# The eleven bf16 data sums of the MID node, on GpSimd or on VectorE

## The chip, the cores and the metric

The kernel runs on one core of one Trainium2 chip. The metric is the device time of one launch in microseconds (us). "Before" ran at 779.34 us, the median of 2 runs (779.1 to 779.57). Each run has a state by its granted TensorE clock and its time; only fast runs are compared. A ratio below is the mean time of one kernel's fast runs over the mean of the other's fast runs of the same rounds on the same chip, so it is not quite the ratio of the medians that are quoted.

## The reference, cut to what matters

```python
# x: [8, 4096, 512] f32, kernel: [8, 512, 512] f32
out = np.zeros_like(x)
for k in range(8):
    shifted = x if k == 0 else concatenate([zeros(B, k, D), x[:, :-k]], axis=1)
    out += np.matmul(shifted, kernel[k])
```

It is a causal convolution of eight taps whose weights are 512x512 matrices.

## The kernel before

Each of the 128 partitions holds a run of 256 consecutive time steps, taken in 32 rounds of eight. Eight taps on eight steps would be 64 matrix products. Three nested levels of a Karatsuba-like scheme need fewer. A round has three nodes, MID, LO and HI. Each has nine products of four 128x128 by 128x512 matmuls on sums of input blocks: the D tiles in the code, in bf16. The sums at the level of the data cost no matmul but a pass of an elementwise engine.

```python
    def tt(o, a, b, op):
        nc.vector.tensor_tensor(out=o, in0=a, in1=b, op=op)

    def load(out, src):
        nc.gpsimd.dma_start(out=out, in_=src)        # f32 in HBM to bf16 in SBUF

    def load_x(i, h):                                 # two buffers in all
        xin[i, h] = xpool.tile([P, 4, D], bf, name="xin")
        load(xin[i, h], xr[:, K * i + 4 * h:K * i + 4 * h + 4, :])

    def transpose_x(i, h):
        nc.sync.dma_start_transpose(out=XT[:, 4 * h:4 * h + 4, :]..., in_=xin[i, h]...)

    def prep_m():                                     # MID's D1 (2 sums), D2[1:5] (4 sums)
        tt(D1[:, 0:2], XT[:, 7::-7], XT[:, 0:2], ADD)
        tt(pairs(D2[:, 1:5]), pairs(XT)[:, 3::-3], pairs(XT)[:, 0:2], ADD)

    def prep_d27():                                   # D2[0], 1 sum
        tt(D2[:, 0], XT[:, 5], XT[:, 7], ADD)

    def prep_d21():                                   # D21, 4 sums, MID's last level
        tt(D21[:, 0:4], D2[:, 0:4], D2[:, 1:5], ADD)
    # ... prep_d4, prep_d41, prep_d42, prep_d421: the same for LO and HI
```

The steady loop, one node a pass:

```python
    for k, (i, a) in enumerate(order):                # MID, LO, HI of each i
        # ...
        if a == MID and more:
            transpose_x(i + 1, 0)                     # first transpose of the next round
        node_l(cur, 0, LO)                            # MID: reads D21[0]
        node_l(cur, 0, HI)
        # ... a0 and u products of the next node
        node_l(cur, 1, LO)
        node_e(cur, 0)                                # output: ACT copy in MID, else VectorE + store
        # ... ACT seeds the next node's PSUM banks
        if a == MID:
            prep_d421(LO)
            prep_d41(HI)
        elif a == LO:
            if more:
                prep_m()
            prep_d421(HI)
        elif more:
            prep_d41(LO)
            prep_d42(LO)
            prep_d21()
        # ... v products of the next node, and the two differences (VectorE, PSUM)
        if a == MID:
            prep_d42(HI)
            prep_d27()
        elif more:
            prep_d4(LO if a == LO else HI)
        node_l(cur, 1, HI)
        # ... a1 product of the node after the next: reads D1 when that is MID
        node_e(cur, 1)
        if a == LO and more:
            transpose_x(i + 1, 1)                     # second transpose of the next round
            if i + 2 < NIT:
                load_x(i + 2, 0)                      # overwrites what transpose (i+1, 0) read
                load_x(i + 2, 1)                      # overwrites what transpose (i+1, 1) read
```

Before, GpSimd's queue held only the loads in the steady loop.

Of the kernel before, what the change touches and what calls it, by code (L numbers as in the profile page):

```python
# [22 lines left out]
def kernel(  # L23
# [6 lines left out]
    nc = tc.nc  # L30
# [44 lines left out]
    def tt(o, a, b, op):  # L75
        nc.vector.tensor_tensor(out=o, in0=a, in1=b, op=op)  # L76
# [7 lines left out]
    def load_x(i, h):  # L84
# [4 lines that stand above are left out]
        nc.sync.dma_start_transpose(  # L89
            out=XT[:, 4 * h:4 * h + 4, :].rearrange("p j (c m) -> p (j c) m", m=P),  # L90
            in_=xin[i, h].rearrange("p j d -> p (j d)"))


    def pairs(z):
        return z.rearrange("p (a b) d -> p a (b d)", b=2)

    def prep_m():

        tt(D1[:, 0:2], XT[:, 7::-7], XT[:, 0:2], ADD)
        tt(pairs(D2[:, 1:5]), pairs(XT)[:, 3::-3], pairs(XT)[:, 0:2], ADD)  # L100

    def prep_d27():
        tt(D2[:, 0], XT[:, 5], XT[:, 7], ADD)

    def prep_d21():
        tt(D21[:, 0:4], D2[:, 0:4], D2[:, 1:5], ADD)

    def prep_d4(h):
        a, b = (XT[:, 4:8], XT[:, 0:4]) if h == LO else (XT[:, 0:4], XT[:, 4:8])
        tt(D4[:, 4 * h:4 * h + 4], a, b, ADD)  # L110

    def prep_d41(h):
        if h == LO:
            tt(D41[:, 0:2], D4[:, 7::-7], D4[:, 0:2], ADD)
        else:
            tt(D41[:, 2:4], D4[:, 3:5], D4[:, 4:6], ADD)

    def prep_d42(h):
        if h == LO:
            tt(pairs(D42)[:, 0:2], pairs(D4)[:, 3::-3], pairs(D4)[:, 0:2], ADD)  # L120
        else:
            tt(D42[:, 4:8], D4[:, 2:6], D4[:, 4:8], ADD)

    def prep_d421(h):
        if h == LO:
            tt(D421[:, 0:4:2], D42[:, 7:0:-6], D42[:, 0:4:2], ADD)
            tt(D421[:, 1:4:2], D42[:, 0:4:2], D42[:, 1:4:2], ADD)
        else:
            tt(D421[:, 4:8], D42[:, 3:7], D42[:, 4:8], ADD)
# [106 lines left out]
    def node_a1(k):  # L236
        n = Node()
        nodes.append(n)
        n.k, (n.i, n.a) = k, order[k]
        a = n.a  # L240
        n.s = streams(n.i, a)
        n.q = pair(3)
        product(n.q[:, 1], n.s[1][1], W[a, MID, HI], True)
        nc.scalar.copy(out=n.q[:, 0], in_=n.q[:, 1])  # L244
        n.p = {}

    def node_a0(n):
        product(n.q[:, 0], n.s[1][0], W[n.a, MID, LO], False)

    def node_u(n):  # L250
        product(n.q[:, 1], n.s[0], W[n.a, MID, MID], False)

    def node_seed(n, b_):
        n.p[b_] = pair((2 * n.k + b_) % 3)
        if b_ == LO:
            nc.scalar.copy(out=n.p[b_][:, 1], in_=n.q[:, 1])  # L256
        else:
            nc.scalar.mul(out=n.p[b_][:, 1], in_=n.q[:, 1], mul=-1.0)  # L258

    def node_dts(n):  # L260
        n.dts = cpool.tile([P, D], f32, name="dts")
        nc.scalar.copy(out=n.dts, in_=n.q[:, 0])  # L262

    def node_v(n, b_):
        product(n.p[b_][:, 1], n.s[2][b_], W[n.a, b_, MID], False)

    def node_d(n, b_):
        p = n.p[b_]
        if b_ == LO:
            tt(p[:, 0], n.dts, p[:, 1], SUB)  # L270
        else:
            nc.vector.scalar_tensor_tensor(out=p[:, 0], in0=p[:, 1], scalar=-1.0,  # L272
                                           in1=n.dts, op0=MUL, op1=SUB)
# [3 lines left out]
    def node_l(n, b_, j):  # L277
        product(n.p[b_][:, j], n.s[3][2 * b_ + j], W[n.a, b_, j], False)
# [11 lines left out]
    def node_e(n, b_):  # L290
        p = n.p[b_]
        if n.k < 4:
            pool, name = ((mpool, "ms"), (ypool, "y"), (fpool, "f"), (ypool, "y"))[n.k]
            y = pool.tile([P, 2, D], f32, name=name)
            nc.scalar.copy(out=y, in_=p)  # L295
            first[n.i, n.a, b_] = y
        elif n.a == MID:
            ms[b_] = mpool.tile([P, 2, D], f32, name="ms")
            nc.scalar.copy(out=ms[b_], in_=p)  # L299
        else:  # L300
            y = ypool.tile([P, 2, D], f32, name="y")
            if b_ == HI and n.k == len(order) - 1:

                for j, eng in enumerate((nc.scalar, nc.sync)):
                    tt(y[:, j], p[:, j], ms[b_][:, j], ADD if n.a == LO else SUB)
                    eng.dma_start(out=orr[:, K * n.i + 4 * n.a + 2 * b_ + j, :], in_=y[:, j])
            else:
                tt(y, p, ms[b_], ADD if n.a == LO else SUB)
                store(n.i, n.a, b_, y)
# [111 lines left out]
    node_u(nodes[1])  # L421
    node_e(nodes[0], 0)
    prep_d27()
    mid_dve(2, HI, LO)
    load_w(1)
# [88 lines left out]
    node_l(nodes[4], 0, LO)  # L514
    node_u(nodes[5])
    prep_m()
    node_d(nodes[4], 1)
    node_y(nodes[4], 0, LO)
# [8 lines left out]
    node_dts(nodes[5])  # L527
    node_v(nodes[5], 0)
    prep_d27()
    node_seed(nodes[5], 1)  # L530
    node_y(nodes[4], 1, LO)
# [42 lines left out]
    for k, (i, a) in enumerate(order):  # L574
        if k < 6:
            continue
        cur = nodes[k]
        more = i + 1 < NIT
        if a == MID and more:
            transpose_x(i + 1, 0)  # L580
        node_l(cur, 0, LO)
        node_l(cur, 0, HI)
        nxt = nodes[k + 1] if k + 1 < len(order) else None
        if nxt:
            node_a0(nxt)
            node_u(nxt)
        node_l(cur, 1, LO)
        node_e(cur, 0)
        if nxt:
            node_seed(nxt, 0)  # L590
            node_seed(nxt, 1)
            node_dts(nxt)
        if a == MID:
            prep_d421(LO)
            prep_d41(HI)
        elif a == LO:
            if more:
                prep_m()
            prep_d421(HI)
        elif more:  # L600
            prep_d41(LO)
            prep_d42(LO)
            prep_d21()
        if nxt:
            for b_ in range(2):
                node_v(nxt, b_)
                node_d(nxt, b_)
        if a == MID:
            prep_d42(HI)
            prep_d27()  # L610
        elif more:
            prep_d4(LO if a == LO else HI)
        node_l(cur, 1, HI)
        if k + 2 < len(order):
            node_a1(k + 2)
        node_e(cur, 1)
        if a == LO and more:
            transpose_x(i + 1, 1)
            if i + 2 < NIT:
                load_x(i + 2, 0)  # L620
                load_x(i + 2, 1)
# [30 lines left out]
```

## Time and profile before

| | before |
|---|---|
| time | 779.34 us |
| TensorE busy | 99% |
| VectorE busy | 85% |
| GpSimd busy | 5% |
| granted TensorE clock | 1.00 |
| a steady round | 23.32 us |

Busy shares say which engine has no room; they don't say which wait ends last. For this, read the chain that ended last and the waits. A row of groups reads: line, engine, operation, output from input, shapes, count, then busy us and the mean ns of one, then the idle time ahead of it and what ended that. Rows in order of time begin with the start and the duration. Three rows of before to compare with later, from the groups with shapes kept apart; these are the bf16 sums of VectorE of 2048 and 1024 elements a partition, and its outputs, which read one operand from PSUM:

```profile
L76 DVE TENSOR_TENSOR D<-D 128x2048 bf16<-128x2048 bf16 x123 | 147.3, 1217 | 0.0
L76 DVE TENSOR_TENSOR y<-pp,ms 128x1024 f32<-128x1024 f32 x119 | 145.2, 1221 | 45.0 <-PE pp L197 44.9
...
L76 DVE TENSOR_TENSOR D<-D 128x1024 bf16<-128x1024 bf16 x127 | 81.8, 682 | 1.6 <-ACT D L353 1.6
```

Nothing disturbs them: 1.22 us and 0.68 us each.

### The profile page before, as it was taken

The page shows a single profiled execution, that of the slowest core. Times are in us where ns is not written, and L with a number is a line of the kernel's source. Part 1 is how long each engine was busy: PE and PEld are TensorE (multiplying, and loading weights), DVE is VectorE, ACT ScalarE, POOL GpSimd, SP SyncE. Part 2 cuts the span into 40 slices and gives each one's busy share as a digit, 9 for nine tenths or more (in the row PEclk, how much of TensorE's full clock was granted, in tenths as well). Part 3 has the DMA queues.
Part 4 walks back from the last instruction along what each step waited for, and adds up shares of the span by engine and source line. Part 5 has one row for each costly group of instructions (what it writes and reads, how often), then busy time and mean ns, then how long its engine had stood idle before and what let it go on. Part 6 is the DMA issues. An engine that isn't in the chain of part 4 may idle for free.

```text
span 777.3 us, 9450 instructions
## 1 busy us (share of the span) xinstructions
PE 766.8 (99%) x3584; PEld 347.3 (45%) x3584; DVE 657.5 (85%) x766; ACT 284.9 (37%) x462; POOL 42.3 (5%) x80
## 2 busy tenths in 40 slices
PE   7999999999999999999999999999999999999997
PEld 3444444444444444444444444444444444444443
DVE  4999988898888898888898888898888898888895
ACT  3553343333343333343333343333343333343332
POOL 4000000000000000000000000000000000000000
PEclk9999999999999999999999999999999999999999
DMA  9986878868786877787877878877697867687843
GB/s 199 211 125 170 226 185 178 208 159 190 164 199 163 197 172 189 164 198 169 194 171 187 164 174 190 207 162 188 163 187 176 207 158 190 165 186 179 204 133 121
DMA packets 159373, 139.42 MB, mean 179 GB/s; under 512 B 130144, under 2 KB 134240, under 8 KB 159200
## 3 DMA queue, kind: packets, MB, share of 16 engines
q1 hardware_dynamic: 145456, 99.89, 46.1%
q0 software_dynamic: 13728, 38.67, 31.6%
q8 instruction: 28, 0.46, 0.2%
q10 hardware_dynamic: 144, 0.26, 0.1%
q14 instruction: 17, 0.14, 0.1%
HBM read 77.33 MB, written 67.11 MB: 186 GB/s over the span
## 4 chain that ended last, share of the span: by engine, by line
PE 96%; DMA 2%; POOL 1%; ACT 0%; issue 0%; DVE 0%; DVEq 0%; POOLq 0%
PE pp L197 96%; DMA xin<-in_x_dram 2%; POOL w L80 0%; PE pp L186 0%; ACT y L295 0%; DVE y L76 0%; DVE pp L76 0%; POOL xin L80 0%; DVEq L647 0%; ACT pp L256 0%; ACT pp L244 0%; POOL XT L80 0%; PE pp L180 0%; POOL ident masks.py:199 0%; POOL ident masks.py:197 0%
## 5 line engine op out<-in xcount | busy, mean ns | idle before, releaser
L197 PE MATMUL pp<-w,D 128*128 128x512 bf16 x3280 | 715.5, 379 | 1.3 <-DVE w L76 0.9
L197 PEld LDWEIGHTS <-D 128*128 128x128 bf16 x3280 | 320.4, 98 | 389.8 <-issue 2.8
L76 DVE TENSOR_TENSOR D<-D 128x1024 bf16<-128x1024 bf16 (+1 forms) x252 | 228.2, 945 | 1.6 <-ACT D L353 1.6
L76 DVE TENSOR_TENSOR y<-pp,ms 128x1024 f32<-128x1024 f32 (+1 forms) x121 | 146.5, 1212 | 45.5 <-PE pp L197 45.4
L76 DVE TENSOR_TENSOR D<-XT 128x2048 bf16<-128x2048 bf16 (+2 forms) x153 | 142.1, 946 | 8.5 <-DMA XT<-xin 6.7
L244 ACT COPY pp<-pp 128x512 f32<-128x512 f32 x95 | 54.1, 570 | 256.0 <-PE pp L197 256.0
L256 ACT COPY pp<-pp 128x512 f32<-128x512 f32 x95 | 54.1, 570 | 170.6 <-PE pp L197 167.6
L76 DVE TENSOR_TENSOR pp<-dts,pp 128x512 f32<-128x512 f32 x95 | 65.5, 690 | 46.2 <-ACT dts L262 44.6
L299 ACT COPY ms<-pp 128x1024 f32<-128x1024 f32 x60 | 61.0, 1016 | 33.1 <-PE pp L197 33.1
L80 POOL DMA_DIRECT2D xin<-in_x_dram x64 | 34.2, 535 | 688.3 <-DMA XT<-xin 670.6
L272 DVE SCALAR_TENSOR_TENSOR pp<-pp,dts 128x512 f32<-128x512 f32 x95 | 65.9, 693 | 3.2
L262 ACT COPY dts<-pp 128x512 f32<-128x512 f32 x95 | 57.4, 604 | 2.0 <-PE pp L197 2.0
L258 ACT ACTIVATE pp<-pp 128x512 f32<-128x512 f32 x95 | 56.0, 589 | 1.2 <-DVE y L76 1.2
L197 PE MATMUL pp<-w,XT 128*128 128x512 bf16 x120 | 30.8, 379 | 0.0
L76 DVE TENSOR_TENSOR w<-w,w 128x2048 bf16<-128x2048 bf16 x18 | 21.6, 1219 | 0.4 <-DMA w<-in_kernel_dram 0.2
L197 PEld LDWEIGHTS <-XT 128*128 128x128 bf16 x120 | 11.7, 98 | 14.2
L180 PE MATMUL pp<-zero 128*128 128x512 bf16 x24 | 8.9, 505 | 2.4 <-DVE zero L145 1.2
L197 PE MATMUL pp<-w,w 128*128 128x512 bf16 x36 | 9.0, 379 | 1.3 <-ACT pp L244 0.7
L197 PE MATMUL pp<-w,F 128*128 128x512 bf16 x36 | 8.9, 379 | 0.0
L338 DVE MEMSET D<- 128x64 bf16 x2 | 0.2, 112 | 8.2 <-ACT D L351 7.7
L80 POOL DMA_DIRECT2D w<-in_kernel_dram x8 | 6.0, 766 | 0.8 <-DMA w<-in_kernel_dram 0.8
L197 PEld LDWEIGHTS <-w 128*128 128x128 bf16 x36 | 3.5, 97 | 5.8 <-issue 2.1
(55 smaller groups left out, 70.6 us busy)
## 6 DMA issues: line engine op xcount, KB each, us to landing
out_dram<-y SPq DMA_DIRECT2D x123, 512.0 KB, 3.5
xin<-in_x_dram POOLq DMA_DIRECT2D x64, 512.0 KB, 5.9
w<-in_kernel_dram POOLq DMA_DIRECT2D x8, 512.0 KB, 15.9
D<-in_x_dram SPq DMA_DIRECT2D x1, 1024.0 KB, 4.9
out_dram<-ms SPq DMA_DIRECT2D x2, 512.0 KB, 4.2
out_dram<-f SPq DMA_DIRECT2D x2, 512.0 KB, 3.7
XT<-xin SPq DMA_TRANSPOSE x61, 6.1
w<-w POOLq DMA_DIRECT2D x1, 512.0 KB, 9.9
```

Source lines behind the costliest of these rows:

```text
L76: nc.vector.tensor_tensor(out=o, in0=a, in1=b, op=op)
L80: nc.gpsimd.dma_start(out=out, in_=src)
L180: nc.tensor.matmul(pw[:, h], lhsT=zero[:, 0:P], rhs=zero, start=True, stop=True)
L197: nc.tensor.matmul(bank, lhsT=comp[:, c * P:(c + 1) * P], rhs=w[:, c, :], start=start and c == 0, stop=c == DC - 1, skip_group_check=True)
L244: nc.scalar.copy(out=n.q[:, 0], in_=n.q[:, 1])
L256: nc.scalar.copy(out=n.p[b_][:, 1], in_=n.q[:, 1])
L258: nc.scalar.mul(out=n.p[b_][:, 1], in_=n.q[:, 1], mul=-1.0)
L262: nc.scalar.copy(out=n.dts, in_=n.q[:, 0])
L272: nc.vector.scalar_tensor_tensor(out=p[:, 0], in0=p[:, 1], scalar=-1.0, in1=n.dts, op0=MUL, op1=SUB)
L299: nc.scalar.copy(out=ms[b_], in_=p)
L338: nc.vector.memset(z[:, :, 0:D:G], 0.0)
```

## The change

Its intent is to relieve VectorE, which is 85% busy, with an engine that looks 95% idle. The sums and their place in the program stay; only the engine of MID's eleven changes, in the steady loop.

```diff
+    def tg(o, a, b, op):
+        nc.gpsimd.tensor_tensor(out=o, in0=a, in1=b, op=op)
+
-    def prep_m():
+    def prep_m(tt=tt):
         tt(D1[:, 0:2], XT[:, 7::-7], XT[:, 0:2], ADD)
         tt(pairs(D2[:, 1:5]), pairs(XT)[:, 3::-3], pairs(XT)[:, 0:2], ADD)
     # ... the same for prep_d27 and prep_d21
         elif a == LO:
             if more:
-                prep_m()
+                prep_m(tg)
             prep_d421(HI)
         elif more:
             prep_d41(LO)
             prep_d42(LO)
-            prep_d21()
+            prep_d21(tg)
     # ...
         if a == MID:
             prep_d42(HI)
-            prep_d27()
+            prep_d27(tg)
```

## The prediction

> **What bounds the kernel now.** I read the busy shares first, then the chain that ended last, then the totals of who waited for whom, and last the instructions of one round in order of time. The page of the kernel before, busy time by engine and the chain by line:
>
> ```profile
> PE 766.8 (99%) x3584; PEld 347.3 (45%) x3584; DVE 657.5 (85%) x766; ACT 284.9 (37%) x462; POOL 42.3 (5%) x80
> ...
> PE pp L197 96%; DMA xin<-in_x_dram 2%; POOL w L80 0%; PE pp L186 0%; ACT y L295 0%; DVE y L76 0%; DVE pp L76 0%; POOL xin L80 0%; DVEq L647 0%; ACT pp L256 0%; ACT pp L244 0%; POOL XT L80 0%; PE pp L180 0%; POOL ident masks.py:199 0%; POOL ident masks.py:197 0%
> ```
>
> TensorE carries the end: 96% of the chain is its products at L197. [...]the 100 us from 400 to 500 hold 465 matmuls, 0.215 us each, back to back at a granted clock of 1.00. A node has 9 products of 4 matmuls, a round of three nodes (MID, LO, HI) 108, so 108 x 0.215 = 23.2 us; the XT products of two rounds stand at 422.80 and 446.12, 23.32 us apart. There are 30 steady rounds (i = 2 to 31). VectorE is full but not the bound. So **lifting work off VectorE has nothing to win**: not 2% of the span is TensorE waiting. The change can only be neutral or hurt.
>
> Next, what GpSimd is doing. The totals of waits:
>
> ```profile
> POOL xin L80 <- DMA XT<-xin: 670.6, 59, 15.6
> ```
>
> GpSimd looks idle (5%), but it isn't free: its queue stands 670.6 us, 59 times, at the load of the next input block, which may overwrite its buffer only when the transposing DMA has read it. Whatever follows a load in that queue waits with it. Instructions in order of time, one round, VectorE, GpSimd and SyncE (start, duration, engine):
>
> ```profile
> 415.50 1.82 DVE L76 TENSOR_TENSOR D<-XT 128x1024 bf16<-128x1024 bf16 x2
> ...
> 419.57 1.21 DVE L76 TENSOR_TENSOR D<-XT 128x2048 bf16<-128x2048 bf16 x1
> ...
> 420.70 1.22 DVE L76 TENSOR_TENSOR y<-pp,ms 128x1024 f32<-128x1024 f32 x1
> ...
> 422.38 3.26 SPq L89 DMA_TRANSPOSE XT<-xin  x1
> ...
> 423.28 2.95 DVE L76 TENSOR_TENSOR D<-D 128x1024 bf16<-128x1024 bf16 x3
> ...
> 427.50 1.23 DVE L76 TENSOR_TENSOR D<-XT 128x2048 bf16<-128x2048 bf16 x1
> 427.94 0.53 POOL L80 DMA_DIRECT2D xin<-in_x_dram  x1 [12.81 <-DMA XT<-xin]
> ```
>
> By program order: 415.50 is prep_m (D1, D2) in LO; 420.70 LO's last output; 422.38 the second transpose; the three sums at 423.28 are HI's d41, d42 and, last, D21, done at 426.2; 427.94 is the second load. Its transpose landed 5.0 us after 422.38 by the view of that DMA, at 427.4; the load is over at 428.47, 1.1 us after the landing.
>
> Where are the nodes? TensorE uses XT only in the fourth product of HI, at 422.80, so HI starts at 422.80 - 3 x 0.864 = 420.2 and the next MID at 420.2 + 7.77 = **428.0**. MID's first product reads D21.
>
> [...]
>
> **The change part by part.** Counted per round, over 29 rounds (D21 made in HI of 2 to 30).
> Removed from VectorE: D1 0.68, D2 1.22, D21 1.22, D2[0] 0.42 = 3.54 us of some 20. Off the path: worth 0, except that prep_m's 1.82 us stood before LO's last output. That output's products end at HI's start less the a1 product, 420.2 - 0.86 = 419.3; it started at 420.70. So it and the transpose behind it may come at most about 1.1 us earlier.
> [...]
> Moved, and this is the step that decides: the order in GpSimd's queue is prep_m, load, load, D21, D2[0]. prep_m can start when the first transpose lands (414.1)[...]; the a1 product wants D1 at 419.3 and HI's v products want D2 from 424.5.[...] But D21, which VectorE had done at 426.2 before that second transpose landed, now stands **behind the second load**, so behind the landing[...]. MID is 5.0 us late. Nothing absorbs it: the next second transpose is issued behind LO's last output, which is behind MID, so the lateness is paid in every round. Loop: 15.5 us for MID and LO, 2.2 to the transpose, 5.0 landing, 1.1 load[...].
> Further terms: up to -1.1, taken as -0.5, for the earlier output[...]; +1.0 for the clock[...].[...]
> 5.0 - 0.5 + 0.3 + 1.0 = 5.8 us; x 29 = 168; 779 + 168 = **947 us**.
>
> **Rivals.**
> (a) GpSimd is fast on bf16, or D21 is hidden: [...]Then 2.8 + 0.3 - 0.5 and no clock loss = 2.6 x 29 = 75, 855 us. To come out even D21 would have to take under 0.6 us and TensorE wait for nothing.[...]
> (b) [...]That would be about +6.7 x 29 = 195, 975 us; partly the same time as the stall above, so not added. For it: VectorE is 86% busy.[...]
> (c) VectorE was the hidden pacer and is freed: against it, TensorE has no idle time to give.
>
> **Range and chances.** The stall's existence rests on queue order and a landing, both in the trace; its size on the duration of D21, which I know least. D21 at 3 us without clock loss gives (3.5 - 0.5 + 0.3) x 29 = 96, 875[...]. Range 870 to 1030, point 947. Faster 0.01, within 2% 0.03, slower 0.96.
>
> **What would show each step.** TensorE busy share near 80%, with 29 waits of some 4 to 6 us on GpSimd's D21 at L197; rounds near 29 us; the chain no longer TensorE but alternating transpose, load, GpSimd, TensorE; GpSimd's D21 beginning some 1.1 us after the landing; clock below 1.00 in part of the rounds; VectorE's SBUF sums lengthened or late when GpSimd runs, PSUM ones not. Wrong if GpSimd's 2048 sum takes under 2 or over 6 us, if the load no longer waits for the transpose[...].

In the sum 5.0 - 0.5 + 0.3 + 1.0, D21's length on GpSimd, which is part of the 5.0, the 0.3 us for a hold-up of D21 by a sum of VectorE and the 1.0 us for the clock are the author's estimates, which the trace of before could not show: no sum ran on GpSimd there, and the clock is 1.00 in all of its steady rounds. Rivals (a) and (b), the second that GpSimd's sums and VectorE's hold each other up, and the ends of the range are priced by such estimates too. What the later traces show of each stands below.

## The result, and the profile after

The changed kernel took 989.46 us, the median of 2 runs (988.8 to 990.13), against 779.34: ratio 1.2695, 95% interval 1.2659 to 1.2732. The profiled run was fast.

Busy times, and the chain by engine and line, of the kernel after:

```profile
PE 841.2 (85%) x3513; PEld 363.9 (37%) x3584; DVE 710.1 (72%) x649; ACT 285.6 (29%) x462; POOL 386.6 (39%) x197
...
PE 61%; DMA 17%; POOL 14%; DVE 4%; issue 3%; SPq 1%; ACT 0%; POOLq 0%; DVEq 0%
PE pp L199 61%; DMA XT<-xin 15%; POOL D L98 12%; DVE y L76 4%; DMA xin<-in_x_dram 2%; POOL xin L80 2%; SPq L284 1%; POOL w L80 0%; PE pp L188 0%; DVE D L76 0%; SPq L89 0%; ACT y L297 0%; DVE pp L76 0%; DVEq L649 0%; ACT pp L258 0%
```

TensorE no longer carries the end alone. The chain goes through the transposing DMA, GpSimd and its load. VectorE has fewer instructions (649 against 766) and yet more busy time, 710 us against 657. The totals of waits of the kernel after:

```profile
PE pp L199 <- POOL D L98: 129.3, 28, 8.8
```

There are 28 waits of TensorE on GpSimd, 4.6 us each in the mean; before there were none. Here is the end of one steady round of the kernel after and the start of the next, in order of time, with the rows that matter (a number in brackets is the idle time ahead, and who ended it):

```profile
528.50 3.24 SPq L89 DMA_TRANSPOSE XT<-xin  x1
...
529.13 1.03 PE L199 MATMUL pp<-w,XT 128*128 128x512 bf16 x4
...
534.01 0.53 POOL L80 DMA_DIRECT2D xin<-in_x_dram  x1 [15.01 <-PE pp L199]
534.56 4.15 POOL L98 TENSOR_TENSOR D<-D 128x2048 bf16<-128x2048 bf16 x1
...
534.71 1.22 DVE L76 TENSOR_TENSOR y<-pp,ms 128x1024 f32<-128x1024 f32 x1
535.84 5.57 DVE L76 TENSOR_TENSOR D<-D 128x1024 bf16<-128x1024 bf16 x3
...
538.76 21.15 PE L199 MATMUL pp<-w,D 128*128 128x512 bf16 x82 [4.29 <-POOL D L98]
538.78 1.48 POOL L98 TENSOR_TENSOR D<-XT 128x512 bf16<-128x512 bf16 x1
```

Read it downwards. The second transpose is issued at 528.50 and lands 5.0 us later (the view of that DMA), at 533.5. The second load, for which it had to land, follows at 534.01, and D21 only behind that, at 534.56. D21 ends at 538.71, and TensorE, idle for 4.29 us, begins MID at 538.76. The 15.01 us that GpSimd idled ahead of the load are put down to TensorE in this row; the wait that mattered is the landing half a microsecond before it.

The busy time and the clock of the same kernel in three stretches, from the wait of the round before to the next load (after each engine's busy time: PEclk, the granted clock; DMA share; GB/s):

```profile
503.90:508.20 4.30, 0.09 (x1) 0.00 (x0) 4.30 (x3) 0.57 (x1) 4.28 (x2) 0.86 0.80 142
508.20:513.80 5.60, 5.55 (x14) 1.97 (x15) 2.70 (x3) 1.01 (x1) 2.93 (x2) 0.50 0.68 178
513.80:534.40 20.60, 20.50 (x94) 9.20 (x94) 14.22 (x15) 6.81 (x12) 5.59 (x4) 1.00 0.48 127
```

In the wait TensorE is idle. For the 5.6 us behind it the clock is **0.50**: some 13 matmuls in the time of 26, which loses 2.8 us. Then it is 1.00 again. So a round is 30.5 us (D21 starts at 504.05 and 534.56) against 23.3: 4.3 waiting, 2.8 at half clock and 0.1 left over. This holds for the whole run: the trace's records of the granted clock have one spell at half clock at each of the 28 waits, 27 of 6.83 us and one of 10.24. In all, 152 us of matmuls fall into them, which loses 76 us; with the 129 us of waiting that is 205 of the 210 us.

The sums of VectorE and GpSimd in the kernel after, by group:

```profile
L76 DVE TENSOR_TENSOR D<-D 128x1024 bf16<-128x1024 bf16 x127 | 184.9, 1493 | 1.6 <-ACT D L355 1.6
L76 DVE TENSOR_TENSOR D<-D 128x2048 bf16<-128x2048 bf16 x94 | 145.3, 1545 | 0.0
L76 DVE TENSOR_TENSOR y<-pp,ms 128x1024 f32<-128x1024 f32 x119 | 145.2, 1221 | 39.0 <-PE pp L199 37.9 <-remote 1.1
L98 POOL TENSOR_TENSOR D<-D 128x2048 bf16<-128x2048 bf16 x29 | 121.0, 4174 | 0.5
L98 POOL TENSOR_TENSOR D<-XT 128x2048 bf16<-128x2048 bf16 x29 | 118.8, 4096 | 0.0
```

VectorE's sums from SBUF grew from 0.68 to 1.49 us and from 1.22 to 1.55; its outputs, which read PSUM, still take 1.22. D21 and D2 take 4.1 to 4.2 us on GpSimd, 3.4 times VectorE's time.

**The trace holds an experiment of its own.** D21 is made 29 times, but TensorE waits on it 28 times. In round 30 there is no load any more between D2 and D21, since no further input is left. GpSimd's rows of that round:

```profile
941.90 6.14 POOL L98 TENSOR_TENSOR D<-XT 128x1024 bf16<-128x1024 bf16 x2 [2.43 <-DMA XT<-xin]
...
948.12 4.93 POOL L98 TENSOR_TENSOR D<-D 128x2048 bf16<-128x2048 bf16 x1
```

D21 starts right behind D2, and TensorE doesn't wait for it.

### The profile page after: what moved, and what is told of

It is laid out like the page before. It is cut to its first block, busy times and chain, and to the rows that moved or that the text cites. A ratio compares the mean times of both kernels' runs of the same rounds, so it can differ in the third digit from the quotient of the medians.

```text
span 987.0 us, 9440 instructions
## 1 busy us (share of the span) xinstructions
PE 841.2 (85%) x3513; PEld 363.9 (37%) x3584; DVE 710.1 (72%) x649; ACT 285.6 (29%) x462; POOL 386.6 (39%) x197
## 4 chain that ended last, share of the span: by engine, by line
PE 61%; DMA 17%; POOL 14%; DVE 4%; issue 3%; SPq 1%; ACT 0%; POOLq 0%; DVEq 0%
PE pp L199 61%; DMA XT<-xin 15%; POOL D L98 12%; DVE y L76 4%; DMA xin<-in_x_dram 2%; POOL xin L80 2%; SPq L284 1%; POOL w L80 0%; PE pp L188 0%; DVE D L76 0%; SPq L89 0%; ACT y L297 0%; DVE pp L76 0%; DVEq L649 0%; ACT pp L258 0%
## 5 line engine op out<-in xcount | busy, mean ns | idle before, releaser
L199 PE MATMUL pp<-w,D 128*128 128x512 bf16 x3214 | 790.2, 407 | 135.3 <-POOL D L98 129.3
L199 PEld LDWEIGHTS <-D 128*128 128x128 bf16 x3280 | 337.0, 104 | 582.5 <-POOL D L98 142.8
L76 DVE TENSOR_TENSOR D<-D 128x1024 bf16<-128x1024 bf16 (+1 forms) x223 | 329.4, 1510 | 1.6 <-ACT D L355 1.6
L98 POOL TENSOR_TENSOR D<-XT 128x512 bf16<-128x512 bf16 (+2 forms) x88 | 223.8, 2557 | 111.6 <-DMA XT<-xin 96.4
L98 POOL TENSOR_TENSOR D<-D 128x2048 bf16<-128x2048 bf16 x29 | 121.0, 4174 | 0.5
L76 DVE TENSOR_TENSOR D<-XT 128x2048 bf16<-128x2048 bf16 (+2 forms) x65 | 79.2, 1221 | 10.9 <-DMA XT<-xin 9.0
L199 PE MATMUL pp<-w,XT 128*128 128x512 bf16 x118 | 30.5, 379 | 0.2
```

Of the source, the lines that this page charges most:

```text
L98: nc.gpsimd.tensor_tensor(out=o, in0=a, in1=b, op=op)
L199: nc.tensor.matmul(bank, lhsT=comp[:, c * P:(c + 1) * P], rhs=w[:, c, :], start=start and c == 0, stop=c == DC - 1, skip_group_check=True)
```

## The experiments

All results were correct against the reference. Two theories stood at the start: **Q**, D21 stands in GpSimd's queue behind the load and so behind the landing; **P**, GpSimd's arithmetic itself costs, by its speed or by holding up VectorE's sums.

| run | GpSimd does | median us | ratio to before (95%) |
|---|---|---|---|
| after | all eleven | 989.46 | 1.2695 (1.2659 to 1.2732) |
| e1 | all but D21 | 860.39 | 1.105 (1.1008 to 1.1091) |
| e2 | D21 only | 987.72 | 1.2668 (1.2649 to 1.2687) |
| e3 | all, load behind D21 | 856.32 | 1.0988 (1.097 to 1.1005) |
| e5 | all, D21 in halves | 913.27 | 1.1698 (1.1668 to 1.1728) |
| e4 | all, 12 idle matmuls | 938.24 | 1.2037 (1.1995 to 1.2079) |
| e10 | all, 6 idle matmuls | 940.3 | 1.2065 (1.2047 to 1.2082) |
| e6 | idle reads only | 932.25 | 1.1965 (1.1925 to 1.2004) |
| e7 | idle writes only | 779.77 | 1.0005 (0.999 to 1.002) |
| e8 | all in 512 pieces, load behind D21 | 903.84, fast run 889.25 | none, three of four runs slow |
| e9 | D1 and D2[0] | 786.27 | 1.0081 (1.0066 to 1.0097) |
| e11 | D21 only, load behind it | 829.32 | 1.0629 (1.0612 to 1.0646) |

### e1: D21 back on VectorE

```diff
-            prep_d21(tg)
+            prep_d21()
```

> Only D21 goes back to VectorE; D1, D2 and D2[0] (seven of the eleven sums, 7.7 of the 11.9 us a round on GpSimd) stay on GpSimd. Theory Q (queue order: D21 stands behind the second load and so behind the landing of the second transpose): the 28 waits of TensorE on GpSimd are gone, time 779 to 800. Rival P (GpSimd's arithmetic itself[...]): two thirds of the GpSimd time is left, so some 120 to 150 of the 210 us stay, 900 to 930.

It took 860.39 us: neither theory's number. Of the 210 us, 129 went with D21 and 81 stayed. The totals of waits of e1 name no wait of TensorE on GpSimd's sums among their longest, but a new one:

```profile
PE pp L199 <- ACT pp L258: 58.3, 49, 3.6
```

and its rows in order of time show where that comes from:

```profile
514.78 6.13 POOL L98 TENSOR_TENSOR D<-XT 128x1024 bf16<-128x1024 bf16 x2 [8.94 <-DMA XT<-xin]
...
516.98 5.01 DVE L76 TENSOR_TENSOR D<-XT 128x2048 bf16<-128x2048 bf16 x1
...
521.92 2.34 DVE L76 TENSOR_TENSOR y<-pp,ms 128x1024 f32<-128x1024 f32 x2
523.22 0.57 ACT L258 COPY pp<-pp 128x512 f32<-128x512 f32 x1 [4.49 <-DVE y L76]
...
523.84 8.43 PE L199 MATMUL pp<-w,D 128*128 128x512 bf16 x36 [1.46 <-ACT pp L258]
```

While D1 and D2 run on GpSimd (514.78 to 520.91), VectorE's D4 sum lasts 5.01 us instead of 1.22 and ends 1.1 us behind them. Its outputs come behind it, so the PSUM bank is free late, ACT seeds it late, and TensorE waits. So Q holds for D21 (its wait is gone), but something else is underneath, of 81 us.

### e2: D21 alone on GpSimd

```diff
-                prep_m(tg)
+                prep_m()
...
-            prep_d27(tg)
+            prep_d27()
```

> Only D21 stays on GpSimd; D1, D2, D2[0] go back to VectorE. Theory Q: the whole loss stays, 970 to 1000, with 28 waits of 4 to 5 us on D21, since D21's place behind the load is unchanged. Rival P: a third of the GpSimd time is left, so about a third of the loss, 840 to 860.

It took 987.72 us: **one instruction of the four carries the whole loss**, as Q says. TensorE waits on it 28 times, 134.9 us:

```profile
PE pp L199 <- POOL D L98: 134.9, 28, 6.5
```

It also says that D1, D2 and D2[0] on GpSimd cost nothing more while that stall is there: their 81 us of e1 are hidden in it.

### e3: all eleven on GpSimd, the second load behind D21

```diff
             prep_d41(LO)
             prep_d42(LO)
             prep_d21(tg)
+            if i + 2 < NIT:
+                load_x(i + 2, 1)
...
                 load_x(i + 2, 0)
-                load_x(i + 2, 1)
```

> All eleven sums stay on GpSimd, the same instructions as the change, but the second load of a round is issued after D21 instead of before it. Theory Q: D21 then starts as soon as D2 is made and is done before MID wants it; the waits on D21 go, time 779 to 830, the upper part if VectorE's sums that are blocked by D1, D2 and D21 delay the differences that LO and HI need. Rival P: [...]the time stays above 900.

It took 856.32 us, above Q's range and below P's. The same instructions in another order are 133 us faster, so most of the change's loss is order, not arithmetic. What is left, 77 us, is close to e1's 81, and it looks the same in the trace: VectorE's 2048 sums from XT take 2.51 us in the mean instead of 1.22.

### e5: D21 in two halves

```diff
-            prep_d21(tg)
+            for j in (0, 2):
+                tg(D21[:, j:j + 2], D2[:, j:j + 2], D2[:, j + 1:j + 3], ADD)
```

> The change, with D21 made in two instructions of 128x1024 each, 2.1 us instead of 4.15. MID's first product needs only the first half. Theory Q[...]: TensorE's wait falls from 4.3 to about 2.3 us a round and the half-speed matmuls after it vanish, 779 + 28 x 2.3 = 843. If the clock loss is proportional to the gap (2.7 us for 4.3 us of gap), 779 + 28 x 3.7 = 883. If D21's length doesn't matter (the wait ends with something else), 985.

It took 913.27 us. The wait behaved: 2.3 to 2.4 us in most rounds (mean 83.0 / 28 = 3.0, as twelve had 2.6 to 6.6). But the matmuls at half clock did not vanish. A wait and the stretch behind it, in e5:

```profile
582.50:584.90 2.40, 0.06 (x2) 0.02 (x2) 2.40 (x3) 0.57 (x1) 2.38 (x3) 1.00 0.66 102
584.90:590.00 5.10, 5.10 (x16) 1.96 (x17) 4.56 (x3) 1.01 (x1) 4.01 (x2) 0.67 1.09 251
590.00:598.00 8.00, 8.00 (x38) 3.60 (x37) 5.87 (x3) 3.08 (x5) 6.66 (x3) 1.00 0.03 6
```

Idle for 2.34 us, TensorE gets a mean clock of 0.67 in the next 5.1 us, that is half clock for 3.4 us: 1.7 us lost to a wait of 2.3. Over the run the mean clock is 0.948, against 0.900 in the kernel after.

Not every wait of this length does this: of the 16 waits of 2.3 to 2.4 us in e5, ten brought a spell at half clock and six none: behind the wait of 2.37 us that ended at 500.07, 84 matmuls took 19.94 us, and behind the one of 2.38 us that ended at 361.20 they took 18.31. The records of the granted clock show where two such waits differ. In the kernel after, all 28 spells start whole multiples of 3.413 us apart, 27 last 6.83 us and one 10.24. Two waits of e5 follow, in stretches of 3.41 us counted from a spell that starts at 585.32: for each, the stretch in which it began and the next one.

```profile
581.91:585.32 3.41, 1.07 (x5) 0.31 (x4) 3.41 (x4) 0.57 (x1) 3.23 (x3) 1.00 0.70 138
585.32:588.73 3.41, 3.41 (x9) 1.18 (x8) 3.41 (x3) 0.60 (x1) 3.41 (x2) 0.50 1.04 263
...
776.47:779.88 3.41, 1.87 (x9) 0.66 (x7) 3.23 (x5) 0.57 (x1) 2.01 (x2) 1.00 0.72 196
779.88:783.29 3.41, 2.62 (x13) 1.21 (x14) 3.41 (x2) 0.68 (x1) 3.41 (x3) 1.00 1.01 235
```

The first wait lies within one stretch, 2.34 us of idle time in 3.41, and the next stretch is at 0.50. The second is as long but lies across a border, 1.54 and 0.79 us, and the next stretch is at 1.00. The kernel after, counted in the same way from 60 us after its start to 30 us before its end, has 204 stretches at full clock. 28 of them were followed by half clock, and these held 2.05 to 3.41 us of idle time on TensorE; the other 176 held at most 0.09 us. All 28 waits brought a spell, so the kernel after pays in every round. This was read from the records afterwards; no run was made to test it, and how the clock is set was not shown.

### e4 and e10: TensorE kept busy in the wait

```diff
+        if a == MID and i > 2:
+            spare = pair((2 * k + 2) % 3)
+            for _ in range(6):            # e10: range(3)
+                fill(spare)               # two matmuls nobody reads
         node_l(cur, 0, LO)
```

> The change, with twelve idle matmuls (2.6 us) on a free PSUM bank ahead of each MID's first product, inside the 4.3 us in which TensorE waits for D21. The data path is untouched. Theory C (of the 7.2 us a round, 4.6 are the wait and some 2.7 are matmuls at half clock, caused by the idle time): the half clock goes, 989 - 28 x 2.7 = 913, between 905 and 925. If the half clock has another cause (say, the array slows by itself), 985 to 990.

> As the run with twelve idle matmuls, but six, since twelve ended 1.5 us after D21 (they ran partly at half clock and began 2 us late). Six take 1.3 us at full clock or 2.6 at half and fit into the wait. Theory C: real matmuls stay at or near full clock, and the overshoot goes: 905 to 925, against 938 with twelve and 989 with none. If the 2 us of idle time ahead of them is enough to halve the clock in most rounds, 940 to 975.

Adding useless work made the kernel **faster**, 989 to 938 us. So the half clock does come from the idle time: the data path is unchanged, and the mean clock rose from 0.900 to 0.979. The expected 913 was missed. The twelve matmuls of e4 can begin only when VectorE's last output frees their bank. In most rounds that is 1.5 us into the wait and they fit: in one they ran from 310.02 to 312.77, and D21 ended at 312.75. But in nine rounds, the first among them, they began 2.0 us or more into the wait and the clock still fell; in the one that e10's expectation goes by they ran mostly at half clock to about 512.5, 1.5 us behind D21. So this overshoot, the reason for e10, was the exception, and with six matmuls the time isn't better. One round of e10:

```profile
508.83 1.46 PE L182 MATMUL pp<-zero 128*128 128x512 bf16 x6 [1.54 <-DVE y L76]
...
511.61 18.53 PE L199 MATMUL pp<-w,D 128*128 128x512 bf16 x82 [1.32 <-POOL D L98]
...
539.65 12.92 PE L199 MATMUL pp<-w,D 128*128 128x512 bf16 x58 [1.32 <-POOL D L98]
```

The clock is 1.00 throughout this round, and it lasts 28.04 us (511.61 to 539.65), 2.5 less than after, which is the clock term. Rounds of this kind alone would make 779 + 28 x 4.7 = 911. Other rounds of e10 last 29 us and more; they make up the rest. The trace names two reasons. The clock still fell to half in six places, with 29 us of matmuls in them, which loses 15 us. And after the first one (5.7 us) five waits ahead of the idle matmuls lasted 3.1 to 3.5 us: in four of these rounds the second transpose landed 5.8 to 6.8 us after its issue instead of 5.0, and in the one that was read (the transpose at 613.79) the load, D21 and VectorE's sum and output, which free the bank, all came behind that landing. The kernel before has such late landings too (6.8 us for the transposes at 235.82 and 538.98) and loses nothing by them. Why they are late was not tested.

### e6 and e7: reads and writes alone

The kernel before, with all its sums on VectorE, and work on GpSimd on which nobody waits. Theory P2 says that VectorE's sums from SBUF stand still while GpSimd reads SBUF; e6 has it read, e7 only write:

```diff
                 load_x(i + 2, 0)
+                wa, wb = W[LO, LO, LO], W[LO, LO, HI]      # e6: reads
+                tg(F21[:, 0:2], wa[:, 0:2], wb[:, 0:2], ADD)
+                tg(F21, wa, wb, ADD)
                 load_x(i + 2, 1)
```

```diff
                 load_x(i + 2, 0)
+                for _ in range(4):                          # e7: writes
+                    nc.gpsimd.memset(F21, 0.0)
                 load_x(i + 2, 1)
```

> The kernel before, all sums on VectorE, plus in each steady round two sums on GpSimd of 128x1024 and 128x2048 bf16, of weights nobody changes into a tile nobody reads, issued behind the first load, so at about the time of D1 and D2 in the run with D21 back on VectorE. No engine waits for them by any data. Theory P2 ([...]VectorE's SBUF sums stand still): 850 to 910, with VectorE's bf16 sums stretched and its sums with a PSUM input not. If the 81 us left in that run came from data waits on D1 and D2, 779 to 785 here.

> As the run with idle reads on GpSimd, but GpSimd fills the tile four times with zeros instead: it writes SBUF for some microseconds a round and reads none. Theory P2, reads alone contend: 779 to 785. If writes or GpSimd's mere being busy did it, the same 850 to 910.

Reads: 932.25 us. Writes: 779.77 us, no loss at all. The rows of the first (e6), then those of the second (e7):

```profile
516.43 0.53 POOL L80 DMA_DIRECT2D xin<-in_x_dram  x1 [8.79 <-DMA XT<-xin]
516.55 8.11 DVE L76 TENSOR_TENSOR D<-XT 128x1024 bf16<-128x1024 bf16 x2
516.97 6.60 POOL L98 TENSOR_TENSOR F<-w,w 128x1024 bf16<-128x1024 bf16 x2
```

```profile
509.03 7.41 POOL L622 MEMSET F<- 128x2048 bf16 x4
509.44 1.82 DVE L76 TENSOR_TENSOR D<-XT 128x1024 bf16<-128x1024 bf16 x2
```

With 6.6 us of reads on GpSimd, VectorE's two sums take 8.11 us; with 7.4 us of writes in the same place they take 1.82, as before. No data ties the two engines here. So **it is GpSimd's reads of SBUF that hold VectorE** here, 8.11 against 1.82 us, while the outputs with a PSUM operand still take 1.22 us in e6. e6 lost more (153 us) than e1 (81). The clock accounts for part of it: 85 us of e6's matmuls and 19 of e1's ran at half clock, which is 42 us lost against 10. For the rest it was argued, not tested, that in e6 VectorE still makes D1 and D2 itself and gets caught with them too.

### e8: each sum a piece of its own

```diff
     def tg(o, a, b, op):
-        nc.gpsimd.tensor_tensor(out=o, in0=a, in1=b, op=op)
+        for j in range(o.shape[1]):
+            nc.gpsimd.tensor_tensor(out=o[:, j], in0=a[:, j], in1=b[:, j], op=op)
# on top of e3; D2[1:5] as four sums as well
```

> All eleven sums on GpSimd with the second load after D21, each sum an instruction of its own of 128x512 (about 1.25 us) instead of 2.1 and 4.1 us. Theory P2[...]: VectorE gets in between pieces, a blocked sum waits about 1 us instead of up to 3.7, so 800 to 835 against 856. If [...]the total of 12 us of GpSimd reads is what counts, 850 to 870.

The one fast run took 889.25 us; three others, at 903 to 911 us, count as slow, so there is no ratio. It isn't the gain that was expected. Pieces cost GpSimd more (416 us of sums in 320 instructions, against 368 in e3), and in the rows VectorE got in between pieces in one place (a 2048 sum in 1.74 us during a string of five) and not in another (two sums took 6.59 us, 1.8 being normal, beside a string of four of 4.48 us). Why one sum got through and the others did not stays open.

### e9 and e11: how much can GpSimd take?

e9 leaves D1 and D2[0] on GpSimd (D2 and D21 on VectorE):

```diff
-    def prep_m(tt=tt):
-        tt(D1[:, 0:2], XT[:, 7::-7], XT[:, 0:2], ADD)
+    def prep_m(tg=tt):
+        tg(D1[:, 0:2], XT[:, 7::-7], XT[:, 0:2], ADD)
...
-            prep_d21(tg)
+            prep_d21()
```

e11 is e2 with e3's order of the load.

> Three of the eleven sums, D1 and D2[0], on GpSimd (some 3.4 us a round), D2 and D21 on VectorE as before. Theory Q+P2: [...]VectorE's D2 begins at most 0.7 us late and takes the place where D1 stood; D2[0] has a round's slack. 779 to 785, the same as before. If any sum on GpSimd costs VectorE its whole length, 3.4 us x 29 less what VectorE gives off (1.1 x 29): 840.

> Only D21 on GpSimd, with the second load after it instead of before: it differs from the run with D21 alone on GpSimd (988) in nothing but that order. Theory Q: D21 starts when VectorE has made D2, near the middle of LO, and is done a node before MID wants it; no wait on it is left. [...]800 to 870. If the order doesn't matter, 988.

e9: 786.27 us, ratio 1.0081 (1.0066 to 1.0097), a trifle slower (the record's bar of 2% calls it the same) and just above what was expected. TensorE has nothing to win from it, and small collisions remain (VectorE's 2048 sum beside D1 took 1.77 us in one round). e11: 829.32 us. Against e2, the order of one load and one sum is worth **158 us**; nothing else differs. D21 now begins right behind D2:

```profile
518.87 4.88 POOL L98 TENSOR_TENSOR D<-D 128x2048 bf16<-128x2048 bf16 x1 [1.39 <-DVE D L76]
...
520.94 3.88 DVE L76 TENSOR_TENSOR D<-XT 128x2048 bf16<-128x2048 bf16 x1
```

Some 50 us are left. Here D21 stretches D4 of LO to 3.88 us, and VectorE's 2048 sums from XT take 2.07 us in the mean instead of 1.22, so GpSimd's reads are the likely cause; that they are all of the 50 us was not shown.

No version that was run beats the kernel before.

## Why the prediction was right, point by point

The time, 989.46 us, lies in the range (870 to 1030), and 42 us above the point of 947. By its own steps:

- **Nothing to win by freeing VectorE: right.** TensorE had no idle time to give. e9 has three sums fewer on VectorE and is 0.8% slower.
- **D21 behind the second load, behind the landing: right, and it is the cause.** D21 was to begin 1.1 us after the landing, and so it did (533.47 to 534.56). e2 against e11 shows the order alone (988 against 829), and round 30, without the load, has no wait.
- **Size of the wait: right.** 5.0 - 0.5 + 0.3 = 4.8 us was summed, with an estimate of D21's length in it; 4.6 was the mean, 4.3 in most rounds, 28 times and not 29, for the reason of round 30. The longest of the others, 6.0 us twice, follow a transpose that landed after 6.7 us; the first wait was 8.8. D21 took 4.17 us, D1 2.12, D2 4.10, D2[0] 1.49 (1.24 in e3).
- **The earlier transpose: smaller than assumed.** HI began 3 x 0.864 ahead of the XT product, at 526.54, the transpose at 528.50: 1.96 us in place of 2.2, a gain of 0.2 where 0.5 was taken.
- **The clock term: the mis-sized one.** The prediction took 1.0 us a round, an estimate that no trace had shown. It was 2.7 us in the mean over all 28 waits (2.8 in the round shown): some 5.5 us of matmuls at half clock, since a spell lasted 6.83 us and most began only 1 to 2 us before the wait ended. This is the term that put the result above the point: (129 + 76) / 29 = 7.1 us a round, of 210 / 29 = 7.2 measured, against 5.8 in the prediction. e4 and e10 show that it hangs on the idle time; with the clock kept, a clean round is 2.5 us shorter.
- **Rival (b), GpSimd's sums and VectorE's hold each other up: real, but not added.** VectorE's bf16 sums grew from 0.68 to 1.49 us and from 1.22 to 1.55. The prediction gave 975 us for this alone, an estimate, and said that it would partly be the same time as the stall. With the stall away it is at most 856 to 860 (e3, e1), so the 975 overstated it; e6, with more sums on VectorE, reached 932. (The rival's 86% for VectorE is 85% on the page.) With the stall it adds nothing that e2 shows (988 without D1, D2 and D2[0] on GpSimd, 989 with them).
- **Rival (a), a fast GpSimd on bf16: wrong.** 2048 bf16 took 4.1 to 4.2 us on GpSimd, against VectorE's 1.22.

Put together, a round after is a loop that closes on itself: 15.5 us of MID and LO + 2.8 clock + 2.0 to the transpose + 5.0 to its landing + 1.1 load + 4.2 D21 = 30.6, against 30.5 measured. The bound of the kernel went over from TensorE to this loop.

What stays open: why some transposes land late; why some of VectorE's sums get through between short GpSimd pieces and others do not (e8); and whether the remaining 0.8% of e9, and all of the 50 us of e11, comes from GpSimd's reads.

## What to carry to other kernels

An engine that is idle isn't free: look at what its queue is waiting for, and put work on it ahead of such a wait, not behind it; the order was worth 158 us here (e2 against e11). Before you split elementwise work between VectorE and GpSimd, count the VectorE instructions that read two SBUF operands: beside 6.6 us of GpSimd's reads two of them took 8.11 us in place of 1.82 (e6), and the versions in a good order still lost 50 to 80 us. And where TensorE is the bound, charge each new wait with the half clock that can follow it, which here was more than half of the wait again (76 us on 129); two waits of 1.5 and 1.3 us with a few matmuls between them mostly went free of it (e10: 1.00 throughout the round shown, half clock in six places of the run).
